# First block's merge: a separate sum tile, five gate buffers, four PSUM banks and squares summed on ScalarE

## Chip, cores and metric

The kernel runs on one core of one Trainium2 chip. The metric is the device time of one execution in microseconds (us), the median of the runs shown; 0.3% of it is 12 us.

## What is computed

Two transformer blocks follow each other on 2048 tokens of width 1024, in float32. The first block projects the tokens, runs two recurrences over them (branches a and b, four heads of 128 each), and merges the branches. The change lies in this merge:

```python
def rms_norm_gated(o, gain, gate):
    o = o * lax.rsqrt(jnp.mean(o * o, axis=-1, keepdims=True) + RMS_EPS) * gain
    return o.reshape(*o.shape[:-2], -1) * jax.nn.silu(gate)

def merge_branches(o_a, o_b, p, ...):
    y_a = rms_norm_gated(o_a, a_norm_l, p['a_gate']) @ w_a_out_l
    y_b = rms_norm_gated(o_b, b_norm_l, p['b_gate']) @ w_b_out_l
    gates = jax.nn.sigmoid(p['merge'].reshape(..., N_BRANCH, D_MODEL))
    return (gates[..., 0, :] * y_a + gates[..., 1, :] * y_b) @ w_out_l
# first block: h = layer_norm(ALPHA * h + gate_l * merge_branches(...)) * ln_g + ln_b
```

## The kernel before

A product in float32 accuracy is made of three passes: both factors are split into a high part and a low rest, and `mm3` issues high by high, high by low and low by high (lines 188 to 190). Every split costs a cast on ScalarE and a subtraction on POOL or VectorE.

The merge goes through the 2048 tokens in eight rounds of 256 (`order`, blocks 7 down to 0; the text counts rounds 0 to 7). A round has three pieces of work.

- `branch(b, j)`, for each half j of 128 tokens of the **next** round: SP loads the recurrences' outputs `o` (L1345, L1346) and the branch gate `sg` (L1348). ScalarE takes SiLU of `sg` (L1349) and squares `o` (L1351), VectorE sums the squares per head (L1354), takes the inverse root by three Newton steps on 128x8 numbers (L177 to L185) and scales `o` (L1356). Its second part, `turned()`, transposes `o` on TensorE (L1362), multiplies by `sg` on VectorE (L1365), and splits the result into `yh` (ScalarE, L1367) and `yl` (VectorE, L1368). `turned()` runs in the middle of the round's output projection.
- `merge(b)`: for each of eight slices m of 128 output columns, SP loads both merge gates `mg` (L1376, 256 KB), ScalarE takes their tanh (L1378), TensorE forms the two branches' products `pp` of 12 matmuls each, and VectorE multiplies each by its gate (L1384) and adds the two (L1386). The sum stays in `mg`. ScalarE casts it to `mh` (L1387), POOL subtracts to get `ml` (L1388). `mg` has three buffers (`MGB`), `pp` two PSUM banks. The text writes the products as (m,s), from (0,0) to (7,1).
- `residual(b, between)`: for each half, SP loads the residual `xt` (L1420, two buffers), TensorE multiplies `mh`/`ml` by `w_out` into `acc` (96 matmuls of 512 columns in a round), VectorE adds the residual (L1428) and normalizes (L1285 to L1292), and SP stores `xt` to `d_h` (L1433).

TensorE's instructions stand in program order from the merge on; those of the other engines are ordered by the framework's scheduler, and each engine, and SP's queue of transfers, runs its list strictly in that order. So an instruction that waits holds up everything behind it on its engine. A buffer that is used again is written only when its last reader is done: the load of `xt` waits for the store of two halves before (same buffer), and the load of an `mg` waits for POOL's L1388 of three slices before. Round 0 also scales, splits and stores away the 16 pieces of `w_out` (L524 to L528), on VectorE, ScalarE and POOL. After round 7 the second block begins.

Of the kernel before, what the change touches and what calls it, by code (L numbers as in the profile page):

```python
# [9 lines left out]
F32 = mybir.dt.float32  # L10
# [4 lines left out]
AF = mybir.ActivationFunctionType  # L15
ALU = mybir.AluOpType
AX = mybir.AxisListType
PSUM = bass.MemoryType.PSUM
# [3 lines left out]
P = 128  # L22
D = 1024
KT = 8
# [30 lines left out]
VB = 2  # L55
DPB = 3
DSP = 0
MGB = 3
QZB = 2
FL = 3  # L60
AHEAD_NS = 20000.0
# [31 lines left out]
def block_kernel(ctx: ExitStack, tc: tile.TileContext, A, out):  # L93
    upto = "z"
    nc = tc.nc
    act, dve, pool, pe, sp = nc.scalar, nc.vector, nc.gpsimd, nc.tensor, nc.sync
# [71 lines left out]
    def small(pl, shape, tag, dtype=F32):  # L168
        return pl.tile(list(shape), dtype, tag=tag, name=tag)

    def rsqrt(pl, v, y, eps, tag, mul=1.0, eng=None):

        e = eng or dve
        shape = list(v.shape)
        h = small(pl, shape, tag + "h")
        z = small(pl, shape, tag + "z")
        e.tensor_scalar(out=z, in0=v, scalar1=float(mul), scalar2=float(eps), op0=ALU.mult, op1=ALU.add)  # L177
        dve.tensor_single_scalar(out=y.bitcast(I32), in_=z.bitcast(I32), scalar=1, op=ALU.logical_shift_right)
        dve.tensor_scalar(out=y.bitcast(I32), in0=y.bitcast(I32), scalar1=-1.0, scalar2=float(0x5F3759DF - 2 ** 31),
                          op0=ALU.mult, op1=ALU.add)  # L180
        e.tensor_scalar_mul(h, z, 0.5)
        for _ in range(3):
            e.tensor_mul(z, y, y)
            e.tensor_mul(z, z, h)
            dve.scalar_tensor_tensor(out=y, in0=z, scalar=1.5, in1=y, op0=ALU.subtract, op1=ALU.mult)  # L185

    def mm3(out, lh, ll, rh, rl, start, stop):
        pe.matmul(out=out, lhsT=lh, rhs=rh, start=start, stop=False)  # L188
        pe.matmul(out=out, lhsT=lh, rhs=rl, start=False, stop=False)  # L189
        pe.matmul(out=out, lhsT=ll, rhs=rh, start=False, stop=stop)  # L190
# [146 lines left out]
    with ExitStack() as s0:  # L337
# [37 lines left out]
        with tc.manual_schedule(engines={mybir.EngineType.SP}):  # L375
            tp = p0t.tile([P, 512], F32, tag="tp", name="tp")
# [25 lines left out]
            for i in range(2):  # L402
                tp = p0t.tile([P, 512], F32, tag="tp", name="tp")
# [5 lines left out]
                for j in range(2):  # L409
                    sp.dma_start(out=d_cs[:, i * 1024:(i + 1) * 1024].rearrange(  # L410
                        "p (m s t) -> p m s t", s=2, t=P)[:, :, j],
                        in_=cst[64 * j:64 * j + 64].rearrange("p (m t) -> p m t", t=P))
# [4 lines left out]
        tp = p0t.tile([P, 512], F32, tag="tp", name="tp")  # L417
        pe.transpose(out=tp[:, 0:113], in_=V, identity=ident[:113, :113])
        dve.tensor_copy(out=VT, in_=tp[:, 0:113])
        tp = p0t.tile([P, 16, 2], F32, tag="tp", name="tp")  # L420
# [906 lines left out]
    with ExitStack() as mctx:  # L1327
# [4 lines left out]
        br = brx.enter_context(tc.tile_pool(name="br", bufs=1))  # L1332
        m1s = mctx.enter_context(tc.tile_pool(name="m1s", bufs=2, space=PSUM, side="right"))
# [5 lines left out]
        def branch(b, j):  # L1339

            i = 2 * b + j
            ts_ = slice(i * P, (i + 1) * P)
            o = br.tile([P, KT, P], F32, tag="o", name="o", bufs=2)
            of = o.rearrange("p k e -> p (k e)")
            sp.dma_start(out=of[:, 0:512], in_=oav[4 * i:4 * i + 4])  # L1345
            sp.dma_start(out=of[:, 512:D], in_=d_ob[i])  # L1346
            sg = br.tile([P, KT, P], F32, tag="sg", name="sg", bufs=2)
            sp.dma_start(out=sg, in_=d_gate[:, 0:8, ts_])  # L1348
            act.activation(out=sg, in_=sg, func=AF.Silu)  # L1349
            sq = br.tile([P, KT, P], F32, tag="sq", name="sq")  # L1350
            act.activation(out=sq, in_=o, func=AF.Square)  # L1351
            ss = br.tile([P, KT], F32, tag="ss", name="ss", bufs=2)
            rs = br.tile([P, KT], F32, tag="rs", name="rs", bufs=2)
            dve.tensor_reduce(out=ss, in_=sq, op=ALU.add, axis=AX.X)  # L1354
            rsqrt(br, ss, rs, 1e-6, "m1r", mul=1.0 / P)
            dve.tensor_tensor(out=o, in0=o, in1=rs.unsqueeze(2).to_broadcast([P, KT, P]), op=ALU.mult)  # L1356

            def turned():
                for s in range(2):
                    tp = m1s.tile([P, 4, P], F32, tag="tp", name="tp")  # L1360
                    for k in range(4):
                        pe.transpose(out=tp[:, k, :], in_=o[:, 4 * s + k, :], identity=ident)  # L1362
                    ks = slice(4 * s, 4 * s + 4)
                    js = slice(j * P, (j + 1) * P)
                    dve.scalar_tensor_tensor(out=sg[:, ks, :], in0=tp, scalar=VT[:, 108 + s:109 + s], in1=sg[:, ks, :],  # L1365
                                             op0=ALU.mult, op1=ALU.mult)
                    act.copy(out=yh[:, ks, js], in_=sg[:, ks, :])  # L1367
                    dve.tensor_sub(yl[:, ks, js], sg[:, ks, :], yh[:, ks, js].bitcast(F32))  # L1368

            return turned  # L1370

        def merge(b):
            for m in range(KT):
                bs = slice(b * 256, (b + 1) * 256)
                mg = m1.tile([P, 2, 256], F32, tag="mg", name="mg", bufs=MGB)
                sp.dma_start(out=mg, in_=d_gate[:, 8 + m:24:8, bs])  # L1376

                act.activation(out=mg, in_=mg, func=AF.Tanh, scale=0.5)  # L1378
                for s in range(2):
                    pp = m1s.tile([P, 512], F32, tag="pp", name="pp")[:, 0:256]  # L1380
                    for k in range(4):
                        mm3(pp, wab[s][0][:, k, m * P:(m + 1) * P], wab[s][1][:, k, m * P:(m + 1) * P],
                            yh[:, 4 * s + k, :], yl[:, 4 * s + k, :], k == 0, k == 3)
                    dve.scalar_tensor_tensor(out=mg[:, s, :], in0=mg[:, s, :], scalar=1.0, in1=pp, op0=ALU.add,  # L1384
                                             op1=ALU.mult)
                dve.tensor_add(mg[:, 0, :], mg[:, 0, :], mg[:, 1, :])  # L1386
                act.copy(out=mh[:, m, :], in_=mg[:, 0, :])  # L1387
                pool.tensor_tensor(out=ml[:, m, :], in0=mg[:, 0, :], in1=mh[:, m, :].bitcast(F32), op=ALU.subtract)  # L1388

        def turn(t, nr, nw, order, w0, tag):  # L1390

            n = nr * nw
            for s in range(2):
                tp = m1s.tile([P, 4, P], F32, tag=tag, name="tp")
                for k in range(4):
                    pe.transpose(out=tp[:, k, :n], in_=t[:n, (4 * s + k) * P:(4 * s + k + 1) * P],
                                 identity=ident[:n, :n])
                src = tp[:, :, :n].rearrange(f"p k {order} -> p k r w", w=nw)[:, :, 0:8]
                dh, dl = (x[:, 4 * s:4 * s + 4].rearrange("p k (r w) -> p k r w", w=GW)[:, :, :, w0:w0 + nw]
                          for x in hT[0])  # L1400
                act.copy(out=dh, in_=src)
                dve.tensor_sub(dl, src, dh.bitcast(F32))
# [36 lines left out]
        for j in range(2):  # L1439
            branch(order[0], j)()  # L1440
# [5 lines left out]
        if upto == "2":  # L1446
            return
        m1 = mctx.enter_context(tc.tile_pool(name="m1", bufs=1, side="right"))
        mh = m1.tile([P, KT, 256], F32R, name="mh")
        ml = m1.tile([P, KT, 256], F32R, name="ml")  # L1450
        gate = m1.tile([P, D], F32, tag="xt", name="gate", bufs=2)
# [8 lines left out]
        for n, b in enumerate(order):  # L1460
            merge(b)
            if n == 0:
                stx.close()
                lnp = mctx.enter_context(tc.tile_pool(name="lnp", bufs=1, side="right"))
                lng = bcast_row(lnp, A["ln_g"][0], D, "lng")
                lnb = bcast_row(lnp, A["ln_b"][0], D, "lnb")
            if n + 1 < len(order):
                between = [branch(order[n + 1], j) for j in range(2)]
            else:

                brx.close()
                wabx.close()
                box["w2"] = hctx.enter_context(tc.tile_pool(name="w2", bufs=W2B))
                wts = load_w2([(0, 416, 0)])
                qz = hctx.enter_context(tc.tile_pool(name="qz", bufs=QZB))
                new_hT(hctx, "hA0", 512, "left")
                between = [lambda: ahead_h((16, 16), (32, 16)), lambda: ahead_h((48, 16), (8, 8))]
            done = residual(b, between)
# [24 lines left out]
    for i in range(4, NT):  # L1503
        t = q1.tile([P, 2, 512], F32, tag="v2", name="h", bufs=VB).rearrange("p a b -> p (a b)")
        sp.dma_start(out=t, in_=d_h[i * P:(i + 1) * P, :])
        tp = q1s.tile([P, 8, 2, 64], F32, tag="sv", name="tp", bufs=1).rearrange("p k a e -> p k (a e)")
# [18 lines left out]
    for i in range(NT):  # L1525
        ps = proj2(i, wts, 416)
        c = q1.tile([P, 512], F32, tag="u", name="c")[:, 0:448]
        ss = small(q1, [P, 2], "ss")
        rs = small(q1, [P, 2], "rsq")
        sq = qz.tile([P, 512], F32, tag="y", name="sq")  # L1530
# [17 lines left out]
        for r0_, r1_, k0, k1 in ((0, P, 0, 3), (64, 96, 3, 4)):  # L1548
            act.copy(out=th[r0_:r1_, k0:k1, :], in_=tr[r0_:r1_, k0:k1, :])
            dve.tensor_sub(tl[r0_:r1_, k0:k1, :], tr[r0_:r1_, k0:k1, :], th[r0_:r1_, k0:k1, :].bitcast(F32))  # L1550
            for t, dd in ((th, d_ch), (tl, d_cl)):
                sp.dma_start(out=dd[r0_:r1_, k0:k1, i * P:(i + 1) * P],
                             in_=t[r0_:r1_, k0:k1, :].bitcast(F32))
# [127 lines left out]
    with ExitStack() as actx:  # L1681
# [39 lines left out]
        for i in range(2):  # L1721
            dve.tensor_scalar(out=kTh[i][96:100].rearrange("p (b c) -> p b c", c=P),
                              in0=ident[96:100].unsqueeze(1).to_broadcast([4, T // P, P]), scalar1=0.0, scalar2=1.0,
# [344 lines left out]
```

## Time and profile before

| | us |
|---|---|
| runs | 3989.38, 3994.24, 3999.57 (median 3994.24) |
| the profiled execution | 3978.06 |
| its span, first to last instruction | 3976.3 |
| TensorE busy | 3577.2 (90%) |
| VectorE busy | 2481.2 (62%) |
| ScalarE busy | 1373.1 (35%) |
| the eight rounds of the merge | 2186 to 2700 of the span |

The profile's page gives the whole span; what a single stage does is read from views that are cut to a stretch of it: who waited for whom, the chain of work that ended last, and the instructions in order of time. In those rows PE is TensorE, DVE is VectorE, ACT is ScalarE, SPq is the sequencer that issues the transfers, and "idle before" with an arrow names what ended the engine's wait.

### The profile page before, as it was taken

The page shows a single profiled execution, that of the slowest core. Times are in us where ns is not written, and L with a number is a line of the kernel's source. Part 1 is how long each engine was busy: PE and PEld are TensorE (multiplying, and loading weights), DVE is VectorE, ACT ScalarE, POOL GpSimd, SP SyncE. Part 2 cuts the span into 40 slices and gives each one's busy share as a digit, 9 for nine tenths or more (in the row PEclk, how much of TensorE's full clock was granted, in tenths as well). Part 3 has the DMA queues.
Part 4 walks back from the last instruction along what each step waited for, and adds up shares of the span by engine and source line. Part 5 has one row for each costly group of instructions (what it writes and reads, how often), then busy time and mean ns, then how long its engine had stood idle before and what let it go on. Part 6 is the DMA issues. An engine that isn't in the chain of part 4 may idle for free.

```text
span 3976.3 us, 57274 instructions
## 1 busy us (share of the span) xinstructions
PE 3577.2 (90%) x18998; PEld 2868.6 (72%) x18998; DVE 2481.2 (62%) x6394; ACT 1373.1 (35%) x3379; POOL 1395.6 (35%) x1666
## 2 busy tenths in 40 slices
PE   4799998888899999988889787878999999999999
PEld 0578877776788887877777677777888765565577
DVE  3645657887776776666665755546405377777766
ACT  0444542221254444444443322212212244444400
POOL 2310124440355555555552311110122246666610
PEclk7899999999999999999999898988999999999999
DMA  5322347763344444544545433324333510001254
GB/s 155 112 61 76 89 139 244 231 183 67 104 135 127 133 130 132 149 136 140 159 142 145 139 103 98 100 88 125 116 103 112 181 47 26 26 18 44 68 170 148
DMA packets 528220, 467.25 MB, mean 118 GB/s; under 512 B 91705, under 2 KB 446371, under 8 KB 527732
## 3 DMA queue, kind: packets, MB, share of 16 engines
q1 hardware_dynamic: 527700, 463.54, 39.3%
q8 instruction: 151, 2.47, 0.3%
q14 instruction: 145, 1.19, 0.1%
q0 software_dynamic: 224, 0.05, 0.0%
HBM read 302.08 MB, written 161.37 MB: 117 GB/s over the span
## 4 chain that ended last, share of the span: by engine, by line
PE 38%; DMA 9%; DVE 8%; issue 4%; ACT 2%; POOL 1%; SPq 0%; DVEq 0%; ACTq 0%; POOLq 0%
PE d L188 4%; PE d L189 4%; PE d L190 4%; PE po L1845 3%; PE acc L188 2%; PE acc L189 2%; PE acc L190 2%; DMA d_h<-xt 2%; PE sx L1782 2%; DMA mg<-d_gate 2%; PE st L1812 2%; PE lv L940 2%; PE st L1813 1%; PE st L1814 1%; DMA o<-d_ob 1%
## 5 line engine op out<-in xcount | busy, mean ns | idle before, releaser
L188 PE MATMUL d<-uBh,whi 128*128 128x512 f32 x832 | 364.2, 438 | 18.3 <-ACT gy L835 13.1
L188 PE MATMUL d<-uAh,whi 128*128 128x512 f32 x832 | 357.9, 430 | 11.6 <-DVE gy L848 6.0
L189 PE MATMUL d<-uAl,whi 128*128 128x512 f32 x832 | 333.9, 401 | 5.8 <-DVE uAl L464 5.8
L189 PE MATMUL d<-uBl,whi 128*128 128x512 f32 x832 | 334.9, 403 | 0.0
L235 POOL TENSOR_TENSOR wlo<-wraw,whi 128x512 fp32r<-128x512 f32 x128 | 168.4, 1316 | 467.9 <-ACT whi L234 442.4
L190 PE MATMUL d<-uAh,wlo 128*128 128x512 f32 x832 | 332.3, 399 | 0.0
L190 PE MATMUL d<-uBh,wlo 128*128 128x512 f32 x832 | 332.3, 399 | 0.0
L1818 ACT ACTIVATE pT<-st 128x512 f32<-128x512 f32 (+1 forms) x320 | 170.0, 532 | 232.2 <-PE st L1814 139.7
L1836 POOL TENSOR_TENSOR acc<-acc,pT 128x512 f32<-128x512 f32 (+1 forms) x168 | 185.9, 1107 | 120.7 <-ACT pT L1818 110.9
L1787 DVE TENSOR_REDUCE mx<-sx 128x1 f32<-128x512 f32 (+3 forms) x288 | 169.4, 616 | 47.5 <-PE sx L1782 29.0
L1388 POOL TENSOR_TENSOR ml<-mg,mh 128x256 fp32r<-128x256 f32 x64 | 57.4, 896 | 395.5 <-ACT mh L1387 305.5
L188 PEld LDWEIGHTS d<-uBh,whi 128*128 128x128 f32 x832 | 161.0, 194 | 43.7 <-ACT gy L835 14.0
L188 PEld LDWEIGHTS d<-uAh,whi 128*128 128x128 f32 x832 | 160.6, 193 | 35.9 <-ACT pre L769 5.1
L190 PEld LDWEIGHTS d<-uBh,wlo 128*128 128x128 f32 x832 | 159.3, 192 | 35.4
L190 PEld LDWEIGHTS d<-uAh,wlo 128*128 128x128 f32 x832 | 159.4, 192 | 33.8
L189 PEld LDWEIGHTS d<-uAl,whi 128*128 128x128 f32 x832 | 160.4, 193 | 26.8 <-DVE uAl L464 6.4
L189 PEld LDWEIGHTS d<-uBl,whi 128*128 128x128 f32 x832 | 161.3, 194 | 20.1 <-DVE uBl L464 0.4
L940 PE MATMUL lv<-R,Yt 128*128 128x128 f32 x576 | 100.2, 298 | 82.1 <-DVE R L975 48.7
L631 DVE SCALAR_TENSOR_TENSOR y<-st,VT,y 128x512 f32<-128x512 f32 (+1 forms) x224 | 165.0, 769 | 4.6
L188 PE MATMUL pp<-yh,w_a_out_h 128*128 128x256 f32 x256 | 84.4, 330 | 91.1 <-DVE mg L1384 89.9
L1845 PE MATMUL po<-pT,v 128*64 128x512 f32 (+3 forms) x640 | 161.0, 562 | 3.3 <-DVE o L1859 3.3
L940 PEld LDWEIGHTS lv<-R,Yt 128*128 128x128 f32 x576 | 81.3, 197 | 110.5 <-DVE R L975 58.2
(593 smaller groups left out, 10620.3 us busy)
## 6 DMA issues: line engine op xcount, KB each, us to landing
wraw<-in_w_in_dram SPq DMA_DIRECT2D x126, 256.0 KB
k<-d_k SPq DMA_DIRECT2D x144, 192.0 KB
d_p<-pre SPq DMA_DIRECT2D x64, 384.0 KB
d_gate<-gy SPq DMA_DIRECT2D x96, 256.0 KB
rows<-d_rows SPq DMA_DIRECT2D x36, 512.0 KB
pr<-d_p SPq DMA_DIRECT2D x128, 128.0 KB
mg<-d_gate SPq DMA_DIRECT2D x64, 256.0 KB
wm<-in_w_mod_dram SPq DMA_DIRECT2D x24, 512.0 KB
```

The lines of the kernel that those rows point to most:

```text
L188: pe.matmul(out=out, lhsT=lh, rhs=rh, start=start, stop=False)
L189: pe.matmul(out=out, lhsT=lh, rhs=rl, start=False, stop=False)
L190: pe.matmul(out=out, lhsT=ll, rhs=rh, start=False, stop=stop)
L235: pool.tensor_tensor(out=lo[:, ks, :n], in0=raw[:, :, :n], in1=hi[:, ks, :n].bitcast(F32), op=ALU.subtract)
L631: dve.scalar_tensor_tensor(out=y[:, :w], in0=st[:, o + j:o + j + w], scalar=tap, in1=y[:, :w], op0=ALU.mult, op1=ALU.add)
L940: pe.matmul(out=lv[:, c], lhsT=a[:, c], rhs=b[:, c], start=True, stop=True)
L1782: pe.matmul(out=ps[:, :w], lhsT=qh[0:96, j * P:(j + 1) * P], rhs=kTh[h % 2][0:96, b * 512:b * 512 + w], start=True, stop=not last)
L1787: dve.tensor_reduce(out=m4[:, j:j + 1] if one else mx[:, j, b:b + 1], in_=ps[:, :w], op=ALU.max, axis=AX.X)
L1812: pe.matmul(out=ps[:, c0:], lhsT=kt_h[0:100, ks], rhs=qh[0:100, c0:], start=True, stop=False)
L1818: act.activation(out=pT[:, c0:], in_=ps[:, c0:], func=AF.Exp, scale=SCALE)
L1836: (dve if on_dve else pool).tensor_tensor(out=acc[:, c0:], in0=src[:, c0:], in1=pT[:, c0:], op=ALU.add)
L1845: pe.matmul(out=po_[h, g][r:r + 64, c0:], lhsT=val[kb][:, vs], rhs=pT_.pop((h, g, kb))[:, c0:], start=kb < 2, stop=kb >= 4 * g + 2, skip_g ...
```

## The change

The sum of the two gated products goes into a tile of its own, `ms`, with two buffers, so that an `mg` is free again after VectorE's addition and not after POOL's subtraction. `mg` gets five buffers for three. `pp` moves to a PSUM pool of its own with four banks for two. The squares are taken per head in eight instructions of 128 columns that add up their output as they go (`accum_out`), in place of one instruction of 1024 columns and VectorE's sum.

```diff
-MGB = 3
+MGB = 5
...
-            sq = br.tile([P, KT, P], F32, tag="sq", name="sq")
-            act.activation(out=sq, in_=o, func=AF.Square)
...
-            dve.tensor_reduce(out=ss, in_=sq, op=ALU.add, axis=AX.X)
+            for k in range(KT):
+                sq = br.tile([P, P], F32, tag="sq", name="sq", bufs=2)
+                act.activation(out=sq, in_=o[:, k, :], func=AF.Square, accum_out=ss[:, k:k + 1])
...
-                    pp = m1s.tile([P, 512], F32, tag="pp", name="pp")[:, 0:256]
+                    pp = m1p.tile([P, 512], F32, tag="pp", name="pp")[:, 0:256]
...
-                dve.tensor_add(mg[:, 0, :], mg[:, 0, :], mg[:, 1, :])
-                act.copy(out=mh[:, m, :], in_=mg[:, 0, :])
-                pool.tensor_tensor(out=ml[:, m, :], in0=mg[:, 0, :], in1=mh[:, m, :].bitcast(F32), op=ALU.subtract)
+                ms = m1.tile([P, 256], F32, tag="ms", name="ms", bufs=2)
+                dve.tensor_add(ms, mg[:, 0, :], mg[:, 1, :])
+                act.copy(out=mh[:, m, :], in_=ms)
+                pool.tensor_tensor(out=ml[:, m, :], in0=ms, in1=mh[:, m, :].bitcast(F32), op=ALU.subtract)
...
-                tp = m1s.tile([P, 4, P], F32, tag=tag, name="tp")
+                tp = (m1p if tag == "pp" else m1s).tile([P, 4, P], F32, tag=tag, name="tp")
...
+        m1p = mctx.enter_context(tc.tile_pool(name="m1p", bufs=4, space=PSUM))
```

The scheduler orders the other engines anew. The places below read the same in every round from 1 to 6.

SP, before, from the gate of slice 3 in round 4 to the residual's second half (the tile numbers tell the buffers' uses apart):

```order
L1376 DMA mg_25552<-d_gate_112 128x2x256
L1433 DMA d_h_100<-xt_25258 4x32x1024
L1376 DMA mg_25586<-d_gate_112 128x2x256
L1420 DMA xt_25776<-in_x_dram 128x1x1024
L1376 DMA mg_25620<-d_gate_112 128x2x256
L1376 DMA mg_25654<-d_gate_112 128x2x256
L1433 DMA d_h_100<-xt_25354 4x32x1024
L1376 DMA mg_25688<-d_gate_112 128x2x256
L1420 DMA xt_25872<-in_x_dram 128x1x1024
```

SP, changed, the same round, whose gates of slices 0 to 4 are loaded during the round before:

```order
L1348 DMA sg_25938<-d_gate_112 128x8x128
L1434 DMA d_h_100<-xt_25423 4x32x1024
L1421 DMA xt_25975<-in_x_dram 128x1x1024
L1376 DMA mg_25790<-d_gate_112 128x2x256
L1376 DMA mg_25825<-d_gate_112 128x2x256
L1376 DMA mg_25860<-d_gate_112 128x2x256
L1434 DMA d_h_100<-xt_25519 4x32x1024
L1376 DMA mg_26167<-d_gate_112 128x2x256
L1376 DMA mg_26202<-d_gate_112 128x2x256
L1421 DMA xt_26071<-in_x_dram 128x1x1024
```

Before, slices 3 to 7 are loaded within the round, on both sides of the first store; now slices 5, 6 and 7 are, all of them behind the first store and the load of `xt`, and ahead of the second store.

ScalarE, before, from the output projection of one round into the next round's merge:

```order
L1367 CAST yh<-sg 128x4x128 x2
L1351 ACTIVATE sq<-o 128x1024
L1349 ACTIVATE sg<-sg 128x1024
L1367 CAST yh<-sg 128x4x128 x2
L1351 ACTIVATE sq<-o 128x1024
L1349 ACTIVATE sg<-sg 128x1024
L1387 CAST mh<-mg 128x256 x2
L1378 ACTIVATE mg<-mg 128x512
L1387 CAST mh<-mg 128x256
L1378 ACTIVATE mg<-mg 128x512
```

ScalarE, changed, the same stretch:

```order
L1367 CAST yh<-sg 128x4x128
L1354 ACTIVATE sq,ss<-o 128x128 x3
L1367 CAST yh<-sg 128x4x128
L1354 ACTIVATE sq,ss<-o 128x128 x5
L1367 CAST yh<-sg 128x4x128
L1349 ACTIVATE sg<-sg 128x1024
L1367 CAST yh<-sg 128x4x128
L1354 ACTIVATE sq,ss<-o 128x128 x8
L1349 ACTIVATE sg<-sg 128x1024
L1388 CAST mh<-ms 128x256
L1378 ACTIVATE mg<-mg 128x512
L1388 CAST mh<-ms 128x256 x2
```

The second cast of each half now stands behind squares, or a SiLU, of the next round's data, and the casts of slices 1 and 2 stand behind the tanh of slice 5.

VectorE, before, in round 4's merge, around the last step of the layer norm of the round before (L1292 on its first half):

```order
L185 SCALAR_TENSOR_TENSOR ln1rs_25330<-ln1rz_25338,ln1rs_25330 128x1
L1384 SCALAR_TENSOR_TENSOR mg_25484<-mg_25484,pp_25487 128x256
L183 TENSOR_TENSOR m1rz_25734<-rs_25731 128x8
L1292 SCALAR_TENSOR_TENSOR xt_25258<-xt_25258,ln1rs_25330,lnb_23648 128x1024
L177 TENSOR_SCALAR ln1rz_25434<-ln1mv_25425 128x1
L1384 SCALAR_TENSOR_TENSOR mg_25484<-mg_25484,pp_25501 128x256
```

VectorE, changed, the same step:

```order
L185 SCALAR_TENSOR_TENSOR ln1rs_25495<-ln1rz_25503,ln1rs_25495 128x1
L183 TENSOR_TENSOR m1rz_25920<-rs_25902 128x8
L1292 SCALAR_TENSOR_TENSOR xt_25423<-xt_25423,ln1rs_25495,lnb_23685 128x1024
L184 TENSOR_TENSOR m1rz_25920<-m1rz_25920,m1rh_25919 128x8
L1429 SCALAR_TENSOR_TENSOR xt_25519<-xt_25519,acc_25522 128x512
L185 SCALAR_TENSOR_TENSOR rs_25902<-m1rz_25920,rs_25902 128x8
L1384 SCALAR_TENSOR_TENSOR mg_25615<-mg_25615,pp_25618 128x256
```

L1292, after which SP can store the half, stood between the gate products of slice 1; now it stands ahead of the first gate product.

The other place on VectorE is the sum of slice 3 (`ms_25751`) in the changed order. It needs a free `ms`, and so the POOL subtraction (now L1389) of slice 1. The gate product (4,1), second on `mg_25755`, stands behind it, and with it the PSUM bank for (6,1):

```order
L1384 SCALAR_TENSOR_TENSOR mg_25720<-mg_25720,pp_25737 128x256
L1384 SCALAR_TENSOR_TENSOR mg_25755<-mg_25755,pp_25758 128x256
L1292 SCALAR_TENSOR_TENSOR xt_25519<-xt_25519,ln1rs_25591,lnb_23685 128x1024
L1387 TENSOR_TENSOR ms_25751<-mg_25720 128x256
L1384 SCALAR_TENSOR_TENSOR mg_25755<-mg_25755,pp_25772 128x256
L1387 TENSOR_TENSOR ms_25786<-mg_25755 128x256
L1384 SCALAR_TENSOR_TENSOR mg_25790<-mg_25790,pp_25793 128x256
```

Before, the sum stayed in `mg`, and L1386 waited for no other engine. ScalarE's cast of slice 1 stands behind the tanh of slice 5, as shown above, so this sum does too.

## Rows read from the trace of the kernel before

**Rows 1.** Waits by engine, merge (2190 to 2676): us in total, times, longest.

```profile
ACT mg L1378 <- DMA mg<-d_gate: 226.9, 42, 11.7
...
PE pp L188 <- DVE mg L1384: 91.8, 33, 10.2
```

**Rows 2.** Waits of SP's queue, 2300 to 2640.

```profile
SPq L1420 <- DMA d_h<-xt: 54.7, 10, 8.4
```

**Rows 3.** Chain of waits, one round (2376 to 2445): start us, us, what.

```profile
2393.13 11.07 DMA d_h<-xt
...
2405.22 8.43 DMA mg<-d_gate
2413.73 0.64 ACT mg L1378
2414.39 0.43 DVE mg L1384
```

**Rows 4.** TensorE in order of time, same round: start, us, instruction, idle before.

```profile
2383.45 0.39 PE L189 MATMUL pp<-yl,w_a_out_h 128*128 128x256 f32 x1 [0.52 <-DVE yl L1368]
...
2386.19 0.28 PE L190 MATMUL pp<-yh,w_b_out_l 128*128 128x256 f32 x1
...
2406.01 0.58 PE L188 MATMUL pp<-yh,w_a_out_h 128*128 128x256 f32 x1 [5.56 <-DVE mg L1384]
...
2414.87 0.58 PE L188 MATMUL pp<-yh,w_a_out_h 128*128 128x256 f32 x1 [4.05 <-DVE mg L1384]
...
2423.00 0.39 PE L188 MATMUL acc<-w_out_h,mh 128*128 128x512 f32 x1
```

**Rows 5.** Windows: PE, PEld, DVE, ACT, POOL busy, PEclk, DMA share, GB/s.

```profile
2225.00:2230.00 5.00, 4.16 (x35) 3.95 (x34) 5.00 (x6) 2.17 (x4) 4.86 (x5) 1.00 0.38 111
2415.00:2420.00 5.00, 5.00 (x24) 5.00 (x25) 1.18 (x3) 0.59 (x2) 1.24 (x2) 0.50 0.35 126
```

**Rows 6.** SP's queue in order of time, same round.

```profile
2374.76 0.36 SPq L1348 DMA_DIRECT2D sg<-d_gate  x1
...
2395.42 0.36 SPq L1376 DMA_DIRECT2D mg<-d_gate  x1
...
2407.13 0.56 SPq L1433 DMA_DIRECT2D d_h<-xt  x1
```

**Rows 7.** ScalarE in order of time, same round.

```profile
2377.77 1.06 ACT L1351 ACTIVATE sq<-o 128x1024 f32<-128x1024 f32 x1 [3.77 <-DMA o<-d_ob]
2379.39 1.06 ACT L1349 ACTIVATE sg<-sg 128x1024 f32<-128x1024 f32 x1 [0.56 <-DMA sg<-d_gate]
...
2404.87 0.63 ACT L1378 ACTIVATE mg<-mg 128x512 f32<-128x512 f32 x1 [7.74 <-DMA mg<-d_gate]
...
2415.91 0.41 ACT L1387 CAST mh<-mg 128x256 fp32r<-128x256 f32 x1 [0.72 <-DVE mg L1386]
```

**Rows 8.** ScalarE in an earlier stage that squares with accumulation.

```profile
250.93 0.28 ACT L646 ACTIVATE sq<-tr 128x128 f32<-128x128 f32 x1 [1.74 <-PE tr L641]
251.10 0.19 ACT L646 ACTIVATION_READ_ACCUMULATOR sq<-tr 128x1 f32 x1
251.19 0.27 ACT L646 ACTIVATE sq<-tr 128x128 f32<-128x128 f32 x1
```

**Rows 9.** VectorE in order of time, same round.

```profile
2378.86 1.22 DVE L1354 TENSOR_REDUCE ss<-sq 128x8 f32<-128x1024 f32 x1 [2.81 <-ACT sq L1351]
...
2383.53 0.69 DVE L1368 TENSOR_TENSOR yl<-sg,yh 128x512 fp32r<-128x512 f32 x1
...
2420.78 0.43 DVE L1386 TENSOR_TENSOR mg<-mg 128x256 f32<-128x256 f32 x1
```

**Rows 10.** POOL in order of time, same round.

```profile
2416.44 0.73 POOL L1388 TENSOR_TENSOR ml<-mg,mh 128x256 fp32r<-128x256 f32 x1 [0.93 <-ACT mh L1387]
```

**Rows 11.** Last round: ScalarE in order of time.

```profile
2655.34 1.29 ACT L1378 ACTIVATE mg<-mg 128x512 f32<-128x512 f32 x2 [11.68 <-DMA mg<-d_gate]
```

**Rows 12.** Last round: TensorE in order of time.

```profile
2676.17 0.39 PE L188 MATMUL acc<-w_out_h,mh 128*128 128x512 f32 x1
```

**Rows 13.** Waits of SP's queue, 2640 to 2720.

```profile
SPq L1319 <- PE pp L190: 11.6, 1, 11.6
```

## Prediction

> **What bounds the kernel now.** I first read which engine is busiest over the whole span: TensorE, at 90%, so only time in which TensorE idles or runs slowly can be won. The program differs from before only in the first block's merge, so I then cut the views to that stage. The waits there [rows 1] show the two lines that matter: TensorE waited 91.8 us in 33 pieces for the gate product L1384, and ScalarE 226.9 us for loads of the merge gates `mg`. The reader should see that the second causes the first: the gate product needs the tanh, the tanh needs the load.
>
> Why the load is late stands in the chain of one round [rows 3]. The store of the previous round's first half is issued at 2393.13 and takes 11.07 us. SP then waits for it, since the load of the residual `xt` goes into the same buffer; this wait costs SP 54.7 us in ten rounds' halves [rows 2]. The `mg` load queued behind is issued only at 2405.22 and takes 8.43 us; tanh 0.64 and gate product 0.43 follow, and TensorE restarts at 2414.87. In order of time [rows 4], TensorE shows two holes in that round, 5.56 and 4.05 us. And after the second it runs slowly: in the 5 us from 2415 its granted clock is 0.50 [rows 5], the 1.2 GHz level, and 24 matmuls fill them, 0.21 us each, where the 22 steps from 2383.45 to 2386.19 took 0.12 each [rows 4]. The output projection starts at 2423.00.
>
> **The change, part by part.** All times are put on this round's clock.
>
> *Squares.* Removed per half: one ScalarE pass of 1.06 us [rows 7] and VectorE's sum of 1.22 [rows 9]. Added: eight pairs at the pitch of the earlier stage, 251.19 − 250.93 = 0.26 [rows 8], so 2.1 us of ScalarE. ScalarE has idle time beside the projection [rows 7], so the work itself costs nothing; where it stands does. The second cast `yh` now stands behind three squares of an `o` that lands at 2377.77 [rows 7]: 2377.8 + 3 × 0.26 + cast (of the size of the subtraction `yl`, 0.69 [rows 9]) + `yl` 0.69 = 2379.9. SP's next `sg` load waits for that `yl` and was issued at 2374.76 [rows 6]; it now comes 5 us later. It landed 4.6 us after issue (SiLU began at 2379.39 [rows 7]), so at 2384.5; SiLU 1.06, cast 0.69, `yl` 0.69 end at about 2386.9, where the last `yl` ended at 2383.53 + 0.69 = 2384.2 [rows 9]. Product (0,1) needs it and started at about 2384.9: **loss 1.9 us** per round at its start. Without the idle time on ScalarE it would be 2.1 us per half more.
>
> *Store.* L1292 now stands ahead of the first gate product, and no `mg` load stands ahead of the store on SP, so the store follows that last `yl` by the short steps and one pass of 1024 columns (nearest row 1.22 [rows 9]): about 2388.7 in place of 2393.13. At 11.07 us it ends at 2399.8, and the `mg` load of slice 5 is issued 1.0 us later, as before [rows 3]: 2400.8.
>
> *Five buffers.* Slices 0 to 4 are in the chip when the round starts. TensorE runs through 12 products, (0,1) to (6,0), at 12 × 0.12 = 1.44 each, from 2386.8 to 2404.1; four banks let it. Then (6,1) needs the bank of (4,1), whose gate product stands behind the sum of slice 3, which needs an `ms`, which needs cast and subtraction of slice 1, and that cast stands behind the tanh of slice 5.
>
> *The wait that is left.* How long does slice 5's load take? Bounds: 4.6 us, as the `sg` load of twice the bytes; and 9.4, as the load issued at 2395.42 behind a store [rows 6], whose tanh began at 2404.87 [rows 7]. I take 8.43 [rows 3], since there too `xt` was just ahead and a store was issued 1.9 us behind (2407.13 [rows 6]). So it lands at 2409.2; tanh 0.64 [rows 3], cast 0.41 [rows 7], subtraction 0.73 [rows 10], sum 0.43 [rows 9], gate product 0.43 [rows 3]: TensorE restarts at 2411.9 after 7.8 us. As after the holes before, I let 24 matmuls run at 0.21 (5.1 us), the last 12 at 0.12 (1.4): the projection starts at 2418.4, in place of 2423.00. **Gain 4.6 us, in rounds 1 to 6: 28 us.** Casts and subtractions of slices 6 and 7 stand behind the next round's tanhs; the projection takes slice k after k eighths, so they have some us of cover.
>
> The Trainium skill, page "DMA: Bandwidth & Descriptors", section "Queues, rings and completion order", says that each DMA engine works through a ring's descriptors in order. By it slice 5 would wait for `xt` and itself only, not for the store behind; as an estimate, 768 KB at the `sg` load's rate take 6.9 us from the issue of `xt`, the restart is 2.5 us earlier, and seven such rounds give 17 us more, a median of 3935. The 9.4 us load that landed as its preceding store did fits that rule, and the 8.43 us one, with a store behind it, speaks against it.
>
> *Last round.* It has no next `o` or `sg`. TensorE's projection started at 2676.17 [rows 12], because slice 7 was loaded behind the second store. Now slices 5 and 6 go out where 3 and 4 did, whose tanhs ran at 2655.34 for 1.29 us [rows 11]; cast, subtraction, sum, gate product (0.41 + 0.73 + 0.43 + 0.43) give 2658.6 with 0.3 for handing over, and 24 matmuls at 0.21 put the projection at 2663.7. **Gain 12.5 us.** It isn't lost behind: the second block's first weight load waits for the last product [rows 13] and moves along.
>
> *Round 0.* VectorE is busy for 5.00 and POOL for 4.86 of 5 us there [rows 5] with the split of `w_out`; banks and buffers don't shorten that. Between −1 and 3, I take **1**.
>
> **Sum:** 28 + 12.5 + 1, about 42. The profiled execution took 3978.06 us, 16 below the median of 3994.24; the same difference on the median gives **3952**. The bounds of the load (6.5 to 9.4 us; only an idle queue gives 4.6) and ±1 us at the round's start make 3 to 7.5 us a round: 3932 to 3968.
>
> **Rivals.** *The load is quick (B).* Slice 5 lands after 4.6 us, the lower bound. That is 3.8 us off each wait, which is then 4 us; if the clock also stays up, 24 × 0.09 = 2.2 more: 6.0 × 6 = 36 more than forecast, **3916**. For: little else is queued. Against: each `mg` load beside a store took 8.4 or more.
>
> *The wait is only moved (C).* Slice 5 lands together with the second store, at about 2413.5: 0.3 to 0.5 us a round remain, 7 of the last round, 2 of round 0: 12 us, **3982**. For: the load at 2395.42 [rows 6] shared a store's landing. Against: that store was ahead of it. [...]
>
> *The start of the round is late (D), the other sign.* The chain from `o` over three squares, `yl`, `sg` and SiLU to the last `yl` is new. If `o` and `sg` land 5 us later each, the last `yl` ends at 2396.5, and store, load and restart move with it, the projection to 2428.0: 5.0 us a round lost, 30 in six, less 13.5 in the last and first rounds: slower by 16, **4010**. It decides as soon as the store is issued after 2393.3, where the gain is gone. For: ScalarE already waited 3.77 us for `o` [rows 7], with other transfers about. Against: it then stands 8 us behind today's.
>
> **Chances.** Main case 0.64, B 0.09, C 0.17, D 0.10. A measurement can tell 0.3%, 12 us: faster than that is below 3982. Main case and B lie there, C on the edge (0.07 faster, 0.10 same), D is split 0.07 slower and 0.03 same: faster 0.80, same 0.13, slower 0.07. The range takes in the main case's own 3932 to 3968, C's 3982 and nearly B: 3918 to 3985.
>
> **What would show it.** Right: the store of `xt` issued about 6 us into the round instead of 10; one TensorE wait of about 8 us per round, ending at (6,1), for 5.56 and 4.05; squares in pairs 0.26 apart; rounds shorter by 4 to 5 us. Wrong: the load of slice 5 landing with the second store (C) or within 5 us (B); the last `yl` later than the first gate product by more than a few us (D); or a new wait in the projection for the casts of slices 6 and 7, which I priced at nothing.

## The result, and the profile after

| | before | changed |
|---|---|---|
| median of the runs, us | 3996.01 (4 runs, 3989.38 to 3999.57) | 3944.96 (4 runs, 3941.57 to 3947.47) |
| the profiled execution, us | 3978.06 | 3943.14 |
| its span, us | 3976.3 | 3941.4 |
| rounds 1 to 6 of the merge, mean us | 63.3 | 58.4 |
| round 7, first product to projection, us | 40.5 | 29.5 |

The ratio is 0.9874, interval 0.9856 to 0.9891: 1.3% faster, a gain of 51 us in the medians. The two profiled executions differ by 35 us only. The one of before was 11 us below the fastest of its own four runs, that of the changed kernel lies among its own. What the other 16 us of scatter are, no trace here shows; the parts below add up to the 35. Against the later runs of the kernel before, whose medians are 3989.5 to 3992.1, the change's median is 45 to 47 us lower.

Who waited, in the whole merge (2190 to 2640; the answers to [rows 1]):

```profile
ACT mg L1378 <- DMA mg<-d_gate: 185.3, 29, 16.9
...
PE pp L188 <- DVE mg L1384: 60.1, 10, 9.0
```

SP's queue, 2300 to 2600 (to [rows 2]):

```profile
SPq L1421 <- DMA d_h<-xt: 60.7, 10, 10.5
```

TensorE's wait for gate products fell from 91.8 us in 33 pieces to 60.1 in 10. SP's wait for the store did not fall at all; it is still there, ten times (before, in the same stretch: 51.4 us, nine times). TensorE in order of time, round 3 (to [rows 4]):

```profile
2371.22 0.28 PE L188 MATMUL pp<-yh,w_a_out_h 128*128 128x256 f32 x1
2372.10 0.39 PE L189 MATMUL pp<-yl,w_a_out_h 128*128 128x256 f32 x1 [0.60 <-DVE yl L1368]
...
2373.52 0.28 PE L188 MATMUL pp<-yh,w_b_out_h 128*128 128x256 f32 x1
...
2398.86 0.58 PE L188 MATMUL pp<-yh,w_b_out_h 128*128 128x256 f32 x1 [7.91 <-DVE mg L1384]
...
2403.82 0.28 PE L188 MATMUL pp<-yh,w_b_out_h 128*128 128x256 f32 x1
...
2405.25 0.39 PE L188 MATMUL acc<-w_out_h,mh 128*128 128x512 f32 x1
```

The round begins at 2371.22, its product (0,1) at 2373.52. In place of holes of 1.44, 5.56 and 4.05 us there is one, of 7.91; the 157th product matmul ends it, which is the first of (6,1). The windows show the clock behind it (to [rows 5]):

```profile
2398.00:2400.00 2.00, 1.14 (x5) 1.14 (x6) 1.90 (x5) 0.87 (x3) 1.15 (x3) 0.50 0.41 129
```

SP's queue in the same round (to [rows 6]):

```profile
2367.55 0.36 SPq L1348 DMA_DIRECT2D sg<-d_gate  x1
...
2375.40 0.54 SPq L1434 DMA_DIRECT2D d_h<-xt  x1
2385.89 0.58 SPq L1421 DMA_DIRECT2D xt<-in_x_dram  x1
2386.57 1.47 SPq L1376 DMA_DIRECT2D mg<-d_gate  x3
2388.14 0.55 SPq L1434 DMA_DIRECT2D d_h<-xt  x1
```

The store leaves 4.2 us into the round (before, 10.5), `xt` follows 10.5 us later, when the store is done, and the gates of slices 5 to 7 right behind. ScalarE in order of time (to [rows 7]):

```profile
2371.20 1.06 ACT L1349 ACTIVATE sg<-sg 128x1024 f32<-128x1024 f32 x1 [0.56 <-DMA sg<-d_gate]
...
2395.78 0.63 ACT L1378 ACTIVATE mg<-mg 128x512 f32<-128x512 f32 x1 [15.82 <-DMA mg<-d_gate]
...
2412.70 1.27 ACT L1378 ACTIVATE mg<-mg 128x512 f32<-128x512 f32 x2 [8.34 <-DMA mg<-d_gate]
2413.88 0.39 ACT L1388 CAST mh<-ms 128x256 fp32r<-128x256 f32 x1
```

Slice 5's tanh starts at 2395.78, 9.2 us after SP began to issue its load. The last two lines are a second chain, which the prediction saw but gave no price: the cast of slice 7 stands behind the tanhs of the **next** round's gates. It ended at 2414.27; the projection, begun at 2405.25, wants it after seven eighths of a half, 9.6 us, so at about 2414.8. Half a microsecond was left. One round later nothing was:

```profile
2473.86 0.50 PE L188 MATMUL acc<-w_out_h,mh 128*128 128x512 f32 x1 [0.40 <-ACT mh L1388]
```

### The profile page after: what moved, and what is told of

Its sections match the earlier page's. It is cut to its first block, busy times and chain, and to the rows that moved or that the text cites. A ratio compares the mean times of both kernels' runs of the same rounds, so it can differ in the third digit from the quotient of the medians.

```text
span 3941.4 us, 57471 instructions
## 1 busy us (share of the span) xinstructions
PE 3567.3 (91%) x18998; PEld 2860.7 (73%) x18998; DVE 2447.4 (62%) x6378; ACT 1395.6 (35%) x3619; POOL 1395.9 (35%) x1666
## 3 DMA queue, kind: packets, MB, share of 16 engines
q1 hardware_dynamic: 527700, 463.54, 39.7%
## 4 chain that ended last, share of the span: by engine, by line
PE 41%; issue 7%; DVE 7%; DMA 5%; ACT 2%; POOL 2%; SPq 0%; DVEq 0%; POOLq 0%; ACTq 0%
PE d L188 5%; PE d L189 5%; PE d L190 5%; PE po L1847 3%; PE acc L190 2%; PE acc L188 2%; PE acc L189 2%; PE sx L1784 2%; PE st L1814 2%; PE lv L940 2%; PE st L1815 1%; PE st L1816 1%; DMA wraw<-in_w_in_dram 1%; DMA mg<-d_gate 1%; DMA raw<-in_w_in_dram 1%
## 5 line engine op out<-in xcount | busy, mean ns | idle before, releaser
L190 PEld LDWEIGHTS d<-uAh,wlo 128*128 128x128 f32 x832 | 160.2, 193 | 34.4
L1389 POOL TENSOR_TENSOR ml<-ms,mh 128x256 fp32r<-128x256 f32 x64 | 53.9, 850 | 356.4 <-ACT mh L1388 354.3
L234 ACT CAST whi<-wraw 128x512 fp32r<-128x512 f32 x128 | 78.3, 612 | 215.3 <-DMA wraw<-in_w_in_dram 161.2
```

## The experiments

Twelve kernels, each compared with the kernel before, whose medians on those chips were 3989.5 to 3992.1. "A round" is the mean of rounds 1 to 6, from the first product of round 1 to that of round 7. The change itself was not run again beside them: a difference of a run to the change crosses two groups of runs, between which the median of the kernel before differs by 4 to 6.5 us. The theory to begin with was the prediction's: a round is as long as the last gate load is late, and the load is late because SP waits ahead of it for a store.

**Five gates alone (e1).** `MGB = 5` in the kernel before.

> The kernel before with only MGB = 5. SP's order is then: mg of slice 5, first store, mg of slice 6, xt, mg of slice 7, so only slice 7 is behind the wait for the store. Theory (the round is set by how late the last gate load is issued behind the xt load that waits for the store): the one hole of any size sits at (6,1) or (7,0), at most 3 us; rounds 1 to 6 take 50 to 54 us (before 63.3, change 58.4); time 3915 to 3945. Rival 1 (all parts of the change are needed: two banks and the sum in mg hold TensorE back): 60 us or more a round, above 3970. Rival 2 (gate loads land late wherever they are issued, for lack of bandwidth): hole of 7 us or more stays, 58 us a round, 3950 to 3970.

Measured: 3973.22, ratio 0.9952 (0.9932 to 0.9972), 62.3 us a round. The holes in the products went as expected, and the projection began 26.8 us into round 3 in place of 40.4. But the gain came back. Waits of that kernel, 2190 to 2640:

```profile
PE acc L188 <- ACT mh L1387: 40.8, 18, 4.1
```

The projection now waited for the casts. The time is that of rival 1, but not its reason: two banks and the sum in `mg` did not hold the products back. None of the three theories had the casts.

**Half squares (e2).** The change with the squares in two pieces of 512 columns and summed on VectorE again:

```diff
-            for k in range(KT):
-                sq = br.tile([P, P], F32, tag="sq", name="sq", bufs=2)
-                act.activation(out=sq, in_=o[:, k, :], func=AF.Square, accum_out=ss[:, k:k + 1])
+            for q in range(2):
+                sq = br.tile([P, 4, P], F32, tag="sq", name="sq")
+                act.activation(out=sq, in_=o[:, 4 * q:4 * q + 4], func=AF.Square)
+                dve.tensor_reduce(out=ss[:, 4 * q:4 * q + 4], in_=sq, op=ALU.add, axis=AX.X)
```

(The old form, one instruction of 1024 columns, was not run beside five gates and the sum.)

> The change, but the squares are taken in two ScalarE instructions of 512 columns and summed on VectorE; SP's order is then as with the old squares: mg of slice 5, first store, mg of slice 6, xt, mg of slice 7. Theory (SP's order decides): no hole above 3 us, rounds 1 to 6 of 50 to 53 us in place of 58.4, time 3900 to 3920. Rival 1 (the squares on ScalarE help by themselves, VectorE being late): slower than the change, above 3950. Rival 2 (bandwidth): the 8 us hole stays, 3940 to 3950.

Measured: 3996.18, ratio 1.0006 (0.9995 to 1.0017), 66.5 us a round: 51 us slower than the change. The projection began early again, 25.7 us into round 3, and then waited 6.06, 2.69 and 2.71 us for `mh`. ScalarE in that projection shows why:

```profile
2429.73 1.26 ACT L1379 ACTIVATE mg<-mg 128x512 f32<-128x512 f32 x2 [9.00 <-DMA mg<-d_gate]
2430.90 0.69 ACT L1389 CAST mh<-ms 128x256 fp32r<-128x256 f32 x2
2435.98 0.63 ACT L1379 ACTIVATE mg<-mg 128x512 f32<-128x512 f32 x1 [4.39 <-DMA mg<-d_gate]
2436.52 0.39 ACT L1389 CAST mh<-ms 128x256 fp32r<-128x256 f32 x1
2445.36 1.27 ACT L1379 ACTIVATE mg<-mg 128x512 f32<-128x512 f32 x2 [8.46 <-DMA mg<-d_gate]
2446.54 0.39 ACT L1389 CAST mh<-ms 128x256 fp32r<-128x256 f32 x1
```

Each cast comes right after a tanh that waited for its load; the last two waited for gates of the round after. VectorE (rival 1) doesn't stand in these waits. The first theory fell here: SP's order had been mended and the time had not.

**SP's order by hand (e3, e4).** The change with the loads written where they should be issued and SP kept in that order in rounds 1 to 7; the twins differ in the place of `xt` alone (and, by the scheduler's hand, in some casts against tanhs).

```diff
-        mctx.enter_context(tc.manual_schedule(engines=PE_ONLY))
+                man.enter_context(tc.manual_schedule(engines=PE_ONLY | {mybir.EngineType.SP}))
...
+                if XFIRST and m == 0:
+                    load_xt(2 * b)
+                if m + MGB < len(ahead):
+                    load_mg(*ahead[m + MGB])
+                if not XFIRST and m == 2:
+                    load_xt(2 * b)
```

> The change, with SP's order in rounds 1 to 7 written out: first store, mg of slices 5, 6 and 7, then xt, second store. Squares, banks, ms as in the change. Theory: slice 5 is issued about 8 to 10 us into the round instead of 30 and lands before TensorE needs it; no hole above 3 us; rounds 1 to 6 of 50 to 53 us; time 3900 to 3920. Rival 2 (bandwidth): three loads beside the store land as late as before, hole of 5 us or more, 3935 or above.

> The twin of the run with SP's order written out, in which only the load of xt stands ahead of the gate loads of slices 5, 6 and 7, as in the change. Theory: a hole of 7 to 9 us per round at (6,1), rounds of 58 to 59 us, time 3940 to 3955, so 35 to 50 us behind its twin. Rival 2 (bandwidth): the twins are within 10 us of each other.

Measured: 4007.82, ratio 1.0041 (1.0023 to 1.0059), 69.1 us a round with the gates first; 3988.17, ratio 0.9998 (0.9983 to 1.0013), 66.0 with `xt` first. Both expectations missed. The second twin was meant to be the change again and was not: from round 2 on it had no hole in the products either. In both, TensorE waited for `mh` (the first: 54.3 us, longest 10.2) and some 6 us a round for the transposes of `o`. As a test of SP's order they tell nothing, since the other engines were put in another order as well; they show once more the wait for the casts.

**Casts on POOL (e5, e6).** New theory: two chains of about the same length bound a round. One is first store, `xt`, gate of slice 5, products. The other is second store, `xt`, the next round's gates, their tanhs, and behind these on ScalarE the casts that the projection needs. If so, taking the casts off ScalarE cuts the second.

```diff
-                act.copy(out=mh[:, m, :], in_=ms)
+                act.copy(out=mh[:, m, :], in_=ms) if b == order[0] else pool.tensor_copy(out=mh[:, m, :], in_=ms)
```

In the change (e5):

> The change, but from the second round on the cast of the sum (mh) is made on POOL and not on ScalarE; SP's order stays as in the change. Theory now (two chains of nearly equal length bound a round: first store, xt, gate of slice 5, and on the other side second store, xt, the next round's gates, whose tanhs stand ahead of the casts of slices 6 and 7 on ScalarE): the casts no longer wait behind a tanh, so the hole moves from (6,1) to (7,0) and ends about 1.5 us earlier, one product less runs at the slow clock after it, and no wait for mh is left in the projection; rounds 55 to 56.5 us in place of 58.4, time 3925 to 3938. Rival (ScalarE's order costs the change nothing, and 0.74 us on POOL is longer than 0.41): 3945 or more.

Measured: 3934.33, ratio 0.9861 (0.9843 to 0.9878), 55.7 us a round. All of it as expected: the hole stands at (7,0), 5.42 us in round 3, and no wait for `mh` is left in the projection.

```profile
2406.69 0.58 PE L188 MATMUL pp<-yh,w_a_out_h 128*128 128x256 f32 x1 [5.42 <-DVE mg L1384]
```

The interval of this ratio overlaps that of the change (0.9856 to 0.9891), so the reading rests on the rounds and on the place of the hole more than on the median. In the run with half squares (e6):

> The run with half squares (slice 5's gate ahead of the store, slice 7's behind xt; 66.3 us a round, with waits for mh in the projection), but the casts from the second round on made on POOL. Theory now: the waits for mh (about 10.5 us a round) and the slow clock after them (about 3.5) go, since casts no longer stand behind tanhs of loads that come late; rounds 51 to 55 us, time 3900 to 3930. Rival (bandwidth: loads beside the stores are late wherever the casts stand): a hole of 5 us or more in the products or the projection, above 3950.

Measured: 3961.53, ratio 0.9925 (0.9906 to 0.9945), 59.8 us a round. The waits for `mh` and the holes in the products went, 35 us of e2 with them, but not the expected 66 to 96. A third wait appeared, at the start of the round:

```profile
2381.47 0.58 PE L188 MATMUL pp<-yh,w_a_out_h 128*128 128x256 f32 x1 [8.23 <-ACT yh L1368]
```

SP there waited 101.7 us in 11 pieces for stores ahead of `xt`; behind the second such wait stand the next round's gates and then its `o`. So each of the three waits could go back to SP standing in front of `xt`. The run with `xt` on another queue, below, is built on e5 and tests that for the hole in the products alone; for this third wait it was not tested.

**Two banks (e7) and three gates (e8).** The change with `bufs=2` for `m1p`, and with `MGB = 3`.

> The change with two banks for the products in place of four. Theory: TensorE stops two products earlier, at (5,1), restarts at the same time and has five products left for three: 2.9 us a round, and 1 to 2 us a round at the start, where VectorE is late; rounds 61 to 63 us, time 3960 to 3980. Rival (the buffers alone make the gain): within 8 us of the change.

> The change with three gate buffers in place of five: slices 3, 4 and 5 are loaded behind xt, 6 and 7 behind the second store. Theory: TensorE stops after 10 products in place of 13 and restarts at the same time, 4.4 us a round more; rounds 61.5 to 64 us, time 3965 to 3990. Rival (the separate sum and the banks make the gain): within 8 us of the change.

Measured: two banks 3979.05, ratio 0.9965 (0.9953 to 0.9978), 62.9 us a round, as expected, though TensorE stopped at (5,0), a product earlier than forecast, for 8.73 us in round 3. Three gates 4009.56, ratio 1.0045 (1.0032 to 1.0058), 68.5 us a round, slower than forecast: it stopped at (5,0) for 11.12 us, and then the projection waited 3.41 for `mh`, which nobody had priced.

**`xt` from ScalarE's queue (e9).** The same as e5, and

```diff
-                sp.dma_start(out=xt, in_=xv[4 * i:4 * i + 4])
+                act.dma_start(out=xt, in_=xv[4 * i:4 * i + 4])
```

> The run with casts on POOL, and the two loads of xt per round issued from ScalarE's queue and not from SP, so that the wait for the store holds up ScalarE, which is idle there, and not SP. SP's order is then: first store, mg of slices 5, 6, 7, second store. Theory (the remaining hole of 5.4 us at (7,0) is slice 5's gate behind the wait for the store on SP): the gates are issued about 9 us earlier, the hole goes or is under 2 us, and no product runs at the slow clock; rounds 50 to 53 us in place of 55.7, time 3900 to 3920. Rival (three gate loads beside the store land as late as now, or the tanhs behind xt's wait on ScalarE take the hole's place): rounds of 55 us or more, 3930 or more.

Measured: **3891.08**, ratio 0.9751 (0.9735 to 0.9768), 48.1 us a round. That is 54 us below the change and 43 below e5, more than expected. SP and ScalarE's queue in round 3, which begins at 2362.27:

```profile
2366.77 0.54 SPq L1434 DMA_DIRECT2D d_h<-xt  x1
2370.86 0.36 SPq L1376 DMA_DIRECT2D mg<-d_gate  x1
...
2377.58 0.54 ACTq L1421 DMA_DIRECT2D xt<-in_x_dram  x1
2378.27 1.97 ACT L1378 ACTIVATE mg<-mg 128x512 f32<-128x512 f32 x3 [8.26 <-DMA mg<-d_gate]
```

The gates are issued while the store runs, 6.7 us ahead of `xt`; when ScalarE has done waiting for the store, the gates have landed and three tanhs run at once. The windows of that round:

```profile
2362.00:2410.00 48.00, 47.32 (x306) 42.89 (x305) 32.81 (x103) 14.20 (x47) 9.82 (x16) 1.00 0.44 133
```

TensorE is busy 47.32 of 48 us at the full clock: no wait of any size is left in the round. The DMA engines carry 133 GB/s there, against 110 in a round of the change (the same bytes in a shorter round), so a limit of bandwidth over the round was not what had held the gates up. Against e5 the gates go out 6.5 us earlier (8.6 us into round 3 for 15.1) and their tanhs start 7.4 us after that issue for 10.5. So the earlier issue is the larger part; that `xt` no longer stands ahead of them in SP's queue may be the rest, which no run separates. The Trainium skill, page "DMA: Bandwidth & Descriptors", section "Issuing engines are not separate DMA queues", says that issuing from several engines saves only the sequencer's time to initiate a transfer, usually small. Here what was saved is for the most part the time that a sequencer **waits** before it can issue; with all that hung on it the edit brought 43 us.

**Sum in the gate (e10), squares alone (e11).** The change without `ms`; and the kernel before with the new squares only.

> The change without the separate sum: the sum stays in the gate's tile, five gate buffers, four banks, squares on ScalarE; SP's order is as in the change. Theory: the separate sum brings nothing here; without it no gate product waits for a free sum tile, so the hole moves from (6,1) to (7,0) as with the casts on POOL; rounds 55.5 to 58.5 us, time 3928 to 3946. Rival (the early release of the gate's buffer is what lets slices 0 to 4 of the next round be loaded in time): waits for mh or gates grow, 3955 or more.

> The kernel before with only the squares summed on ScalarE; SP's order becomes first store, xt, mg of slices 3, 4, 5, second store. Theory: the earlier store helps by 4 us, but all three gates stand behind xt where slice 3 had stood ahead of the store; with two banks and three gates TensorE stops at (4,0) and has more left after it: rounds 63 to 69 us (before 63.3), time 3990 to 4030. Rival (the relief of VectorE, 1.2 us per half, gains by itself): 3975 or less.

Measured: sum in the gate 3983.43, ratio 0.9974 (0.9953 to 0.9994), 63.3 us a round. The theory fell and its rival held. The hole did move to (7,0) and shrank to 4.54 us, but the projection then waited 5.40 for `mh`. SP in that round:

```profile
2397.07 0.56 SPq L1433 DMA_DIRECT2D d_h<-xt  x1
2408.14 0.56 SPq L1420 DMA_DIRECT2D xt<-in_x_dram  x1
2408.80 10.91 SPq L1376 DMA_DIRECT2D mg<-d_gate  x3
2419.80 0.57 SPq L1433 DMA_DIRECT2D d_h<-xt  x1
```

The last of the three gates waits for POOL's subtraction, whose cast stands behind slice 5's tanh, and the second store behind it: 22.7 us after the first, where the change has 12.7. So the separate sum is needed, for the second chain.

Squares alone: 4038.71, ratio 1.0113 (1.0098 to 1.0128), 70.4 us a round, slower even than expected: TensorE waits of 10.58 and 4.66 us for gate products in round 3. No gain from the relief of VectorE shows here; what shows is the changed order, with all three gates behind `xt`.

**The kernel before with both late edits (e12).**

> The kernel before (three gates, two banks, sum in the gate, old squares) with the two edits that made the fastest run: casts on POOL from the second round on, and the loads of xt issued from ScalarE's queue. Theory (SP is free, but with three gates slices 3 to 5 are issued with the first store and land some 9 us later, and with two banks TensorE stops at (4,0)): a hole of 4 to 7 us at (4,0), perhaps a small one near (7,0); rounds 55 to 60 us, time 3930 to 3965, so the change's parts are worth 40 to 70 us there. Rival (once SP is not held up, buffers and banks bring nothing): rounds under 51 us, time under 3910.

Measured: 3993.18, ratio 1.0018 (1.0006 to 1.0031), 65.5 us a round. The holes are where they were expected, 5.94 us at (4,0) and 3.41 at (7,0) in round 3, but the round is longer than the 55 to 60 us forecast, and the two edits bring nothing to the kernel before. Against e9 it is 102 us slower: the change's parts are worth that much with these two edits, twice what they are worth without. ScalarE in round 3 shows that the wait for the store (issued at 2397.38) has moved to it:

```profile
2407.99 0.55 ACTq L1420 DMA_DIRECT2D xt<-in_x_dram  x1
2408.66 2.03 ACT L1378 ACTIVATE mg<-mg 128x512 f32<-128x512 f32 x3 [14.62 <-DMA mg<-d_gate]
```

The tanhs that end the hole at (4,0) stand right behind `xt` on ScalarE. Whether they waited for it or for their gates, issued 0.7 us behind the store, the trace doesn't separate. In e9 the tanhs stand behind `xt` too, but there TensorE has five gates and four banks to run on.

## Why the prediction was right

The forecast was 3952 with 3932 to 3968 for the main case, and 0.8 for faster. The mechanism held. By its own steps, on the profiled executions:

| step | forecast | measured |
|---|---|---|
| rounds 1 to 6 | 6 x 4.6 = 28 | 379.7 - 350.1 = 29.6 |
| last round | 12.5 | 40.5 - 29.5 = 11.1 |
| round 0 (measured with all that is ahead of it) | 1 | 2255.94 - 2255.75 = 0.2 |
| behind the merge | 0 | -6.0 |
| sum | 42 | 34.9 |

- **The sum of the rounds.** It came out right by misses that offset each other. The projection begins 34.4 us into a round, mean of the six, where the forecast had 35.75 (2418.4 - 2382.65): 1.3 us better, since the gates are issued 2.6 us earlier than forecast and slice 5's load then takes 1.0 longer. Against that, round 3 of the kernel before, from which the forecast was made, is 0.7 us longer up to its projection than the mean of the six (40.35 for 39.7), and what follows the projection grew by 0.3. That the total is within 2 us is in part luck.
- **The last round.** Forecast 12.5, measured 11.1. The forecast's own terms, with the 0.3 for handing over, give 2658.9 and not 2658.6, so 12.2.
- **The store.** Forecast 6 us into the round, measured 4.2 (2375.40 - 2371.22). Right, and early. The squares, 0.26 us apart by the forecast, came 0.29 to 0.31 apart.
- **The start of the round.** Forecast 1.9 us lost; (0,1) began 2.3 us after (0,0) (2373.52), as before (2.2). Only round 1 lost about that much (3.9). This step failed. `o` landed 5.9 us ahead of the round and not 4.9, and the `sg` load took 3.65 us (2367.55 to 2371.20) and not 4.6. Rival D, which hung on this step, is out by it.
- **The wait that is left.** Forecast 7.8 us at (6,1), measured 7.91 in round 3 and 6.7 to 9.0 over the six. The place and the reason (sum, cast and tanh of slice 5) are those of the forecast: e5 took the casts away and the hole went to (7,0), where gate and bank alone put it.
- **The load.** Taken at 8.43 from the row; 9.2 measured. It landed 9.9 us after the issue of `xt` (2385.89 to 2395.78). The estimate by the rule of the Trainium skill, page "DMA: Bandwidth & Descriptors", section "Queues, rings and completion order", was 6.9 from that issue; the trace goes against the estimate. Whether the ring's order failed in it or the rate borrowed from the `sg` load, no run separates. The lower bound of 6.5 us in the forecast's range is worked out from no row; the mean measured over the six rounds, 9.4, lies at the upper bound.
- **The slow clock.** Forecast 24 matmuls at 0.21; 21 ran so, to 2403.45.
- **The cover of the casts.** The prediction priced the casts of slices 6 and 7 at nothing, with "some us of cover". They had 0.5 us in round 3 and -0.4 in round 4. It cost next to nothing in the change, but it is why e1, e2 and e10, which mended the first chain, won so little.
- **Behind the merge.** Priced at nothing and failed: from the last round's projection on, the changed kernel takes 6.0 us more (1306.1 against 1300.1). TensorE's waits for the two halves' norms are 7.12 and 5.62 us, where before it was 5.48 once:

```profile
2635.32 0.46 PE L188 MATMUL acc<-w_out_h,mh 128*128 128x512 f32 x1
...
2648.10 1.06 PE L1397 MATMUL tp<-ident,h 128*128 128x128 f32 x8 [1.64 <-DMA h<-d_h]
2651.96 1.41 PE L1397 MATMUL tp<-ident,h 128*128 128x128 f32 x8 [2.79 <-DMA h<-d_h]
...
2674.54 1.97 PE L1397 MATMUL tp<-ident,xt 128*128 128x128 f32 x8 [7.12 <-DVE xt L1292]
...
2682.13 1.94 PE L1397 MATMUL tp<-ident,xt 128*128 128x128 f32 x8 [5.62 <-DVE xt L1292]
```

Ahead of them stand two waits for loads of `h`, 4.4 us together, at a place where the kernel before did not wait; at the next group of transposes that kernel waited 3.94 us for VectorE, and the changed one did not. Why the loads of `h` landed later stays open.

Rival B is out by the load of 9.2 us, rival C by rounds that are 4.9 us shorter. The median's gain of 51 us is 9 above the forecast. Since the profiled steps give 35, and the later medians of the kernel before 45 to 47, this part is put down to the scatter of the kernel before and not to a term of the sum.

What the prediction did not see is how the parts hang together. Each undone alone loses two thirds of the gain or more: banks 34 us, sum 38, squares (with their order) 51, gates 65. Alone, five gates gain 0.5% and the squares lose 1.1%; the banks and the sum were not run alone. They are not four gains to be added; each removes the wait that would otherwise end next.

## What to carry to other kernels

Look at what the wait for a load stands behind: a queue whose first entry waits for a store holds up every independent load behind it. The load that has to wait can be issued by an engine that is idle at that moment, if nothing urgent stands behind it there. And before you shorten one chain, write down the next one with its margin in the same round (here a cast behind tanhs of data for the round after, 0.5 us); when a second chain is that near, buffers added for the first give their gain back. Changes to an engine's work also change the order that a scheduler gives to the others, so read the order again after each.

## What was not expected of the hardware

A gate of 256 KB landed in 2.8 us with nothing ahead of it and in 9.6 right behind a store of 512 KB (e2: issued 2405.51 and 2410.18, tanhs at 2408.30 and 2419.80). `xt` could follow the first store of a round after 10.5 us (2375.40 to 2385.89 in the changed kernel), the second after 13.9 (2388.14 to 2402.09). In e9 the round moved more per microsecond than in the change, 133 GB/s against 110, and TensorE waited for none of its gate products in rounds 1 to 7: the place in the queue made a load late, more than the traffic of the round as a whole.
